# A 480-byte tile at the right edge of SBUF moves 14 expert weight buffers to multiples of 512 bytes

## The chip, the cores and the metric

One Trainium2 chip, one core of it. The metric is device time in microseconds (us) of one launch. TensorE, VectorE, ScalarE and GpSimd appear in profiles as PE (PEld for its weight loads), DVE, ACT and POOL; SP is SyncE, which here does nothing but issue DMA transfers and wait for what they need.

## The reference

One layer of a diffusion backbone in float32, with 512 latent tokens and 256 context tokens of width 1024. After a token mixer (Fourier branch, gated recurrent branch, merge, output projection) comes the sub-layer that matters here:

```
scores = softmax(h @ w_router)                      # 512 x 16
g, idx = top_k(scores^T, 64)                        # 64 tokens for each of 16 experts
hid = silu(xg @ w_gate[e]) * (xg @ w_up[e])         # 64 x 1536, w_gate and w_up: 1024 x 1536
out = (hid @ w_down[e]) * g                         # 64 x 1024, w_down: 1536 x 1024
x   = x + g2 * scatter_add(out);  return rmsnorm(x)
```

Each expert has three weight matrices of 6.29 MB, each used once. All 16 experts together read 302 MB.

## The kernel before

**The stages.** Up to 424 us of the profiled execution the kernel does the token mixer, then the output projection and the router (to 482 us), then the 16 experts one after the other (loop at L1160), and at the end the last sums, the norm and four stores (L1222 to L1301).

**The weights as units.** An expert's weights come in 24 units: 8 of `w_gate_e` (128 rows of 1536 floats), 8 of `w_up_e`, 8 of `w_down_e`. A unit is one DMA of 768 KB from HBM into a tile of 128 partitions by 1536 floats, so each partition receives one row of 6144 bytes. The list `units` (L826 to L830) holds 386 of them in the order of use. Only the last nine differ: unit 376 is the gain of the final norm, and 377 to 385 are the last expert's `w_down_e` in column blocks (rows of 2048 bytes in 377 to 380, of 1024 bytes in 381 to 385).

**The buffers.** `eload` (L835) issues the next unit and picks its buffer by the unit's number modulo 22. Buffers 0 to 13 belong to `rings[0]`, a pool opened at L825 on the right side of SBUF, where tiles are placed downward from the edge. Buffers 14 to 18 (`rings[1]`) and 19 (`rings[2]`) lie on the left side; 20 and 21 are two tiles held since before (`wd`, `we`):

```python
NR = (14, 5, 1)
m, i = n % (sum(NR) + 2), 0
while i < 3 and m >= NR[i]:
    m, i = m - NR[i], i + 1
t = rings[i].tile([P, DE], F32, tag="ew", bufs=NR[i], name=f"ew{n}") if i < 3 else held[m]
nc.sync.dma_start(t, src[P * q:P * q + P, :])
```

So in units, 14 transfers to the right ring are followed by 8 to the others, and so on: a turn of 22 units, while an expert takes 24.

**What orders the transfers.** All of them are issued by SP, in the order of `units`. A transfer waits until the unit that was in its buffer 22 units before has been used by TensorE. It also waits for one of eight semaphores in turn (named DMAHW0 to DMAHW7), that is, until the transfer eight before it has landed in all 128 partitions. So at most eight are under way.

**What uses them.** `up_gate` (L1108) multiplies each `w_gate_e` unit into the PSUM tile `G` and each `w_up_e` unit into `U` (L1116), and calls `eload` once per unit. Between units it runs hooks: the scatter of the expert before (L1132), the ranking of the expert two ahead. Odd experts also gather the tokens of the next two (L1088). ScalarE takes the silu of `G` at L1172, once per expert. `w_down_e` is multiplied at L1210, for the last expert at L1267.

**Two waits on ScalarE's queue.** In expert 2 (L1190) and in expert 14 (L1215) ScalarE issues a small DMA into `we` or `g2`. These use the same eight semaphores, so that SP stands until they have landed.

**Where the right ring lies.** Right of it is nothing before the change. The right side ends at byte 229,344 of a partition. The ring's lowest buffer starts at byte 143,328 = 279 x 512 + 480; buffers are 6144 = 12 x 512 bytes long, so all 14 start 480 bytes past a multiple of 512. The eight others start at multiples of 512, between bytes 70,144 and 133,632. The pool `rt` of the router (L865) lies left of the right ring. The four output tiles `os` (L1225) are cut from the right ring too.

Of the kernel before, what the change touches and what calls it, by code (L numbers as in the profile page):

```python
# [9 lines left out]
F32 = mybir.dt.float32  # L10
# [7 lines left out]
P = 128  # L18
# [58 lines left out]
def layer(ctx: ExitStack, tc: tile.TileContext, I, out):  # L77
# [4 lines left out]
    def open_pool(name, bufs=1, side="left", **kw):  # L82
        cm = tc.tile_pool(name=name, bufs=bufs, side=side, **kw)
        p = cm.__enter__()
        return p, lambda: cm.__exit__(None, None, None)

    def sb(name, side="left"):
        return open_pool(name, side=side, reuse_waits="tile")
# [733 lines left out]

    NR = (14, 5, 1)
    rings = [None] * 3
    rings[0], close_ra = sb("ra", "right")  # L825
    units = []  # L826
    for e in range(NE):
# [475 lines left out]
    close_rc()  # L1303
    close_rb()
    close_ra()
    close_stage()
    close_keep()

# [30 lines left out]
```

## Time and profile before

| | us |
|---|---|
| three runs, median | 1206.58 |
| lowest, highest | 1205.19, 1206.61 |
| the profiled execution, its own time | 1205.73 |
| the profiled execution, span from first to last instruction | 1203.9 |
| mean granted TensorE clock | 0.984 |

The span is the time of the profiled execution less 1.8 us that lie around it. All times below are counted from the span's start. The profile gives busy times by engine, the mean rate of the DMA engines by stretch, waits with what ended them, and instructions in order of time.

### The profile page before, as it was taken

The numbers are of one execution on the slowest core, as the hardware profiler recorded it, in microseconds if no ns is written. First come the engines' busy times: TensorE is split into PE (matmuls) and PEld (weight loads), VectorE is DVE, ScalarE is ACT, GpSimd is POOL, SyncE is SP. The second block draws the span as 40 slices with busy tenths as digits, with TensorE's granted clock in tenths as the row PEclk, the third lists the DMA queues.
The fourth block names the chain that finished last, engine by engine and source line by source line (L and its number), as shares of the span: only waits on it lengthen the run. The fifth ranks groups of instructions, "written<-read, shape, count | busy, mean of one in ns | idle before, by whom it ended". The sixth has DMA issues, their size and how long they took to land. (4 is left out here: it accounts for less than half of the span.)

```text
span 1203.9 us, 16716 instructions
## 1 busy us (share of the span) xinstructions
PE 1148.4 (95%) x6891; PEld 684.3 (57%) x6891; DVE 564.3 (47%) x1053; ACT 286.4 (24%) x448; POOL 112.9 (9%) x118
## 2 busy tenths in 40 slices
PE   8979988899999999999999999999999999999986
PEld 5768766588888897545445445445345345345333
DVE  5566899996776675233332332332232232232024
ACT  5443766644322223101001001001001001001004
POOL 5164443310000000000000000000000000000002
PEclk9989988999999999999999999999999999999998
DMA  8922011155555495899899999999999999999995
GB/s 308 300 89 88 18 53 53 35 173 177 188 180 191 149 390 206 313 379 418 356 422 419 418 420 421 418 419 421 420 417 421 421 418 418 422 421 418 419 400 211
DMA packets 115435, 368.01 MB, mean 306 GB/s; under 512 B 8912, under 2 KB 61656, under 8 KB 115232
## 3 DMA queue, kind: packets, MB, share of 16 engines
q1 hardware_dynamic: 112688, 363.52, 76.9%
q0 software_dynamic: 1088, 2.18, 0.6%
q10 hardware_dynamic: 1584, 1.25, 0.4%
q8 instruction: 54, 0.88, 0.3%
q14 instruction: 21, 0.17, 0.0%
HBM read 364.43 MB, written 2.10 MB: 304 GB/s over the span
## 5 line engine op out<-in xcount | busy, mean ns | idle before, releaser
L1116 PE MATMUL U<-ew,g 128*64 128x384 f32 x928 | 167.5, 494 | 8.7 <-DMA ew<-in_w_up_e 8.6
L1116 PE MATMUL G<-ew,g 128*64 128x384 f32 x960 | 171.7, 493 | 3.8 <-DMA ew<-in_w_gate_e 3.5
L1135 DVE TENSOR_TENSOR x<-x,sc 128x512 f32<-128x512 f32 x120 | 77.1, 684 | 104.2 <-PE sc L1132 104.2
L1116 PEld LDWEIGHTS G<-ew,g 128*64 128x64 f32 x960 | 62.8, 136 | 87.0 <-issue 62.6
L1116 PEld LDWEIGHTS U<-ew,g 128*64 128x64 f32 x928 | 60.0, 136 | 90.6 <-issue 56.9
L1247 POOL TENSOR_TENSOR o<-x,ew 128x512 f32<-128x512 f32 (+1 forms) x8 | 7.8, 1003 | 926.7 <-ACT o L1243 926.7
L1213 DVE SCALAR_TENSOR_TENSOR wc<-Y,gc,g 128x512 f32<-128x512 f32 x15 | 11.3, 751 | 148.6 <-PE Y L1210 148.6
L1210 PE MATMUL Y<-ew,wa 128*64 128x512 f32 x312 | 75.7, 598 | 2.2 <-ACT wa L1199 2.2
L1210 PE MATMUL Y<-ew,wd 128*64 128x512 f32 x324 | 77.5, 594 | 0.0
L1199 ACT COPY wa<-T 128x384 f32<-128x384 f32 x16 | 7.7, 479 | 254.2 <-PE T L1198 254.2
L230 DVE TENSOR_TENSOR wL<-raw,wH 128x1024 fp32r<-128x1024 f32 x48 | 62.9, 1341 | 2.0 <-ACT wH L229 1.6
L1172 ACT ACTIVATE wc<-G 128x768 f32<-128x768 f32 x16 | 13.0, 811 | 181.7 <-PE G L1116 181.7
L1210 PEld LDWEIGHTS Y<-ew,wd 128*64 128x64 f32 x324 | 24.2, 137 | 49.1 <-issue 41.7
L1088 PEld LDWEIGHTS xg<-wa,xn 128*128 128x128 f32 x448 | 51.1, 192 | 0.2
L1088 PE MATMUL xg<-wa,xn 128*128 128x128 f32 x448 | 51.2, 275 | 0.0
L1054 DVE TENSOR_SCALAR wc<-wa,score 128x128 bf16<-128x128 f32 (+3 forms) x63 | 24.0, 381 | 56.7 <-ACT wa L1047 56.7
L1210 PEld LDWEIGHTS Y<-ew,wa 128*64 128x64 f32 x312 | 21.8, 136 | 45.0 <-issue 34.6
L1216 ACT CAST wb<-wc 128x512 fp32r<-128x512 f32 x15 | 9.3, 619 | 156.1 <-DVE wc L1213 156.1
L674 PE MATMUL ga<-u,gw 128*128 128x512 f32 x64 | 36.0, 645 | 10.0 <-issue 9.9
L1132 PEld LDWEIGHTS sc<-wb 64*128 64x128 f32 x240 | 23.6, 184 | 35.9 <-issue 35.9
L229 ACT CAST wH<-raw 128x1024 fp32r<-128x1024 f32 x38 | 37.9, 1045 | 17.8 <-PE zO L426 9.9
L699 POOL TENSOR_TENSOR th<-tp,th 128x768 f32<-128x768 f32 x16 | 35.0, 2206 | 49.2 <-DVE tp L698 49.2
(360 smaller groups left out, 2183.9 us busy)
## 6 DMA issues: line engine op xcount, KB each, us to landing
ew<-in_w_gate_e SPq DMA_DIRECT2D x120, 768.0 KB, 14.9
ew<-in_w_up_e SPq DMA_DIRECT2D x116, 768.0 KB, 14.9
ew<-in_w_down_e SPq DMA_DIRECT2D x113, 768.0 KB, 14.9
raw<-in_w_ada SPq DMA_DIRECT2D x24, 1024.0 KB, 5.4
raw<-in_w_in SPq DMA_DIRECT2D x16, 1024.0 KB, 4.9
wd<-in_w_down_e SPq DMA_DIRECT2D x7, 768.0 KB, 12.3
we<-in_w_down_e SPq DMA_DIRECT2D x7, 768.0 KB, 12.9
wd<-in_w_up_e SPq DMA_DIRECT2D x6, 768.0 KB, 14.6
```

The costliest lines, as they stand in the source:

```text
L229: (copy or act.copy)(wH[:, a], raw[:, a])
L230: dve.tensor_sub(wL[:, a], raw[:, a], wH[:, a].bitcast(F32))
L674: pe.matmul(gf[:, 512:1024], gw[:, d, i, :], u[:, TC:TA], start=True, stop=True)
L699: pool.tensor_tensor(b, s, b, op=OP.mult)
L1054: dve.tensor_scalar(GT[c][:, 0:m], sB[:, 0:m], s, None, op0=OP.is_lt)
L1088: pe.matmul(a[k // 4][:, P * (k % 4) + q.start:P * (k % 4) + q.stop], XN[n // 2][:, n % 2, P * k:P * k + P], oh[:, n, q], start=n == 0, st ...
L1116: pe.matmul(t[64 * f:64 * f + 64, n, 0:384], xg[:, k, c:c + CAP], w[:, o:o + 384], start=k == 0, stop=k == KD - 1, tile_position=(0, 64 * f))
L1132: pe.matmul(a[dh][:, c], w, v, start=j == 0, stop=j == 1, tile_position=(64 * dh, 0))
L1135: dve.tensor_add(xs, xs, a[dh])
L1172: act.activation(v3(sl), G[:, :, 0:384], AF.Silu)
L1210: pe.matmul(yp[64 * dh:64 * dh + 64, :], hT[j // 3][:, j % 3, 64 * f:64 * f + 64], w[:, 512 * i:512 * i + 512], start=f == 0 and j == 0, s ...
L1213: dve.scalar_tensor_tensor(y, yp, gc[:, e % 3:e % 3 + 1], g2, op0=OP.mult, op1=OP.mult)
```

## The change

A pool of its own, opened on the right side just before the ring, with one tile of 120 floats (480 bytes) per partition. Nothing reads or writes it.

```diff
     NR = (14, 5, 1)
     rings = [None] * 3
+    edge, close_edge = open_pool("edge", side="right")
+    edge.tile([P, 120], F32, name="edge")
     rings[0], close_ra = sb("ra", "right")
...
     close_ra()
+    close_edge()
     close_stage()
```

The 14 buffers, the pool `rt` and the tiles `os` move 480 bytes down. The lowest buffer now starts at byte 142,848 = 279 x 512, and all 22 buffers start at multiples of 512. No instruction is added, removed or put elsewhere in its engine's order. What lay in that part of SBUF earlier (tiles of the mixer) now borders differently on the ring, and one wait moves. On SP, at the first loads of the right ring (`ew8` is unit 8; the names in brackets are semaphores: of the DMA queue, of TensorE, of GpSimd), before the change:

```order
L861 DMA ew6_3180<-in_w_gate_e 128x1536 [waits DMAHW7_49,PE_49]
L861 DMA ew7_3182<-in_w_gate_e 128x1536 [waits DMAHW0_49]
L861 DMA ew8_3184<-in_w_up_e 128x1536 [waits DMAHW1_49]
L861 DMA ew9_3186<-in_w_up_e 128x1536 [waits DMAHW2_49,PE_49,Pool_49]
L861 DMA ew10_3188<-in_w_up_e 128x1536 [waits DMASW5_49,DMASW4_49,DMASW6_49,DMASW3_49,DMASW7_49,DMASW2_49,DMAHW3_49,DMASW1_49,DMASW0_49]
```

The same place after it, two source lines further down:

```order
L863 DMA ew6_3184<-in_w_gate_e 128x1536 [waits DMAHW7_49,PE_49]
L863 DMA ew7_3186<-in_w_gate_e 128x1536 [waits DMAHW0_49]
L863 DMA ew8_3188<-in_w_up_e 128x1536 [waits DMAHW1_49,PE_49,Pool_49]
L863 DMA ew9_3190<-in_w_up_e 128x1536 [waits DMAHW2_49]
L863 DMA ew10_3192<-in_w_up_e 128x1536 [waits DMASW5_49,DMASW4_49,DMASW6_49,DMASW3_49,DMASW7_49,DMASW2_49,DMAHW3_49,DMASW1_49,DMASW0_49]
```

The wait for the earlier users of that memory on TensorE and GpSimd stands one transfer earlier, at unit 8 in place of unit 9.

## Rows read from the trace of the kernel before

**Rows 1.** The page, parts 1 and 2: busy times, DMA rate in 40 slices.

```profile
PE 1148.4 (95%) x6891; PEld 684.3 (57%) x6891; DVE 564.3 (47%) x1053; ACT 286.4 (24%) x448; POOL 112.9 (9%) x118
...
GB/s 308 300 89 88 18 53 53 35 173 177 188 180 191 149 390 206 313 379 418 356 422 419 418 420 421 418 419 421 420 417 421 421 418 418 422 421 418 419 400 211
```

**Rows 2.** Timeline of ACT, experts 2, 6, 10 and 14: start us, us, instruction.

```profile
589.18 0.81 ACT L1172 ACTIVATE wc<-G 128x768 f32<-128x768 f32 x1 [11.44 <-PE G L1116]
...
756.12 0.81 ACT L1172 ACTIVATE wc<-G 128x768 f32<-128x768 f32 x1 [11.44 <-PE G L1116]
...
932.13 0.81 ACT L1172 ACTIVATE wc<-G 128x768 f32<-128x768 f32 x1 [11.44 <-PE G L1116]
...
1113.11 0.81 ACT L1172 ACTIVATE wc<-G 128x768 f32<-128x768 f32 x1 [11.44 <-PE G L1116]
```

**Rows 3.** Waits of PEld, 602 to 780 us: us in total, times, longest.

```profile
PEld U L1116 <- DMA ew<-in_w_down_e: 0.7, 4, 0.2
```

**Rows 4.** Waits of PEld, 780 to 1172 us, same columns.

```profile
PEld U L1116 <- DMA ew<-in_w_up_e: 30.4, 37, 1.1
...
PEld G L1116 <- DMA ew<-in_w_gate_e: 17.3, 20, 1.5
```

**Rows 5.** Waits of SP's queue, 600 to 1140 us, same columns.

```profile
SPq L861 <- DMA ew<-in_w_gate_e: 128.6, 86, 2.9
```

**Rows 6.** Timeline of SP: start of a group, us to its end, transfers in it.

```profile
628.62 13.56 SPq L861 DMA_DIRECT2D ew<-in_w_gate_e  x8
...
843.40 9.79 SPq L859 DMA_DIRECT2D ew<-in_w_down_e  x6
...
862.25 5.82 SPq L861 DMA_DIRECT2D ew<-in_w_gate_e  x4
...
884.54 13.58 SPq L859 DMA_DIRECT2D ew<-in_w_down_e  x8
...
1126.96 15.47 SPq L861 DMA_DIRECT2D ew<-in_w_gate_e  x8
```

**Rows 7.** Windows of 4 us: busy times, then PEclk, DMA share, GB/s.

```profile
852.00:856.00 4.00, 4.00 (x43) 1.87 (x40) 1.54 (x3) 0.00 (x0) 0.00 (x0) 1.00 1.02 411
856.00:860.00 4.00, 3.83 (x20) 1.80 (x22) 1.45 (x3) 0.88 (x2) 0.00 (x0) 1.00 1.02 419
860.00:864.00 4.00, 4.00 (x18) 1.19 (x14) 0.00 (x0) 0.00 (x0) 0.00 (x0) 1.00 1.01 421
864.00:868.00 4.00, 4.00 (x15) 1.14 (x16) 0.00 (x0) 0.00 (x0) 0.00 (x0) 1.00 1.02 427
868.00:872.00 4.00, 3.69 (x18) 1.10 (x16) 1.51 (x3) 0.62 (x1) 0.00 (x0) 1.00 1.02 427
872.00:876.00 4.00, 3.90 (x28) 1.66 (x26) 1.29 (x2) 0.00 (x0) 0.00 (x0) 1.00 1.01 424
876.00:880.00 4.00, 3.90 (x28) 1.51 (x24) 1.29 (x2) 0.00 (x0) 0.00 (x0) 1.00 1.02 420
880.00:884.00 4.00, 3.85 (x28) 1.52 (x24) 1.28 (x2) 0.00 (x0) 0.00 (x0) 1.00 1.01 415
```

**Rows 8.** Windows of 17.5 us, same columns.

```profile
839.70:857.20 17.50, 17.34 (x128) 8.27 (x126) 8.13 (x20) 2.03 (x4) 0.00 (x0) 1.00 1.02 416
860.20:877.70 17.50, 17.09 (x88) 5.88 (x86) 3.17 (x6) 0.62 (x1) 0.00 (x0) 1.00 1.01 424
```

**Rows 9.** Waits of SP's queue, 540 to 600 us.

```profile
SPq L861 <- DMA we<-g: 13.4, 1, 13.4
```

**Rows 10.** Timeline of SP, 540 to 620 us.

```profile
593.33 3.97 SPq L861 DMA_DIRECT2D ew<-in_w_gate_e  x8
```

**Rows 11.** Timeline of PE, last expert: last unit of up, first of the 1024-byte rows.

```profile
1170.84 1.51 PE L1116 MATMUL U<-ew,g 128*64 128x384 f32 x8 [0.38 <-DMA ew<-in_w_up_e]
...
1182.65 0.83 PE L1267 MATMUL Y<-ew,wa 128*64 128x256 f32 x5 [0.36 <-DMA ew<-in_w_down_e]
```

**Rows 12.** Window between the first loads and the next ones.

```profile
455.00:468.00 13.00, 13.00 (x132) 12.30 (x131) 6.43 (x17) 3.49 (x10) 0.00 (x0) 1.00 0.02 6
```

## The prediction

> **What bounds the kernel now.** I read the page first, then the experts one by one on ScalarE's timeline, then the waits on both sides of the weight transfers, and last the DMA rate in short windows.
>
> The page shows TensorE busy for 95% of the span [rows 1], which looks like a TensorE kernel. The experts' times say otherwise. The silu of the gate comes once per expert, and since odd experts also gather, the experts are to be counted in pairs. From expert 2 to expert 6 it takes 756.12 - 589.18 = 166.94 us, 83.5 us per pair; from expert 10 to 14 it takes 180.98 us, 90.5 us per pair [rows 2]. The same instructions take 7 us more per pair late in the run. The waits say why: between 602 and 780 us the longest of TensorE's weight loads' waits for a DMA is 0.7 us in all, between 780 and 1172 us it is 30.4 us for up and 17.3 us for gate [rows 3, 4]. So TensorE sets the pace until about 780 us, living on what was loaded ahead, and the weight transfers set it from there to the last expert.
>
> The transfers themselves never rest in either stretch. From the 21st slice to the 38th the DMA rate stays at 417 to 422 GB/s [rows 1], and SP, which issues a transfer when the one eight before has landed, waits for landings and for nothing else that matters [rows 5]. So from about 600 us the end of the kernel is the end of the transfers plus a tail: a shorter transfer moves it, and TensorE's floor is 83.5 us per pair against 90.5.
>
> **What a transfer costs by its buffer.** In the steady stretch an issue on SP follows a landing, so the issues' spacing is the landings' spacing. Units 210 to 215 are issued at 843.40 to 853.19 us in a group of six; with 0.33 us for the issue itself that is (9.79 - 0.33) / 5 = 1.89 us apiece, and the landings that release them are of units 202 to 207, buffers 4 to 9 of the right ring. Units 220 to 223 come (5.82 - 0.33) / 3 = 1.83 us apart, released by units 212 to 215, buffers 14 to 17, which lie at multiples of 512 already [rows 6]. So the trace of before contains the experiment: 14 buffers off the multiple land at 1.89 us, 8 buffers on it at 1.83 us. The whole turn, unit 210 to unit 232, takes 884.54 - 843.40 = 41.14 us [rows 6].
>
> But the landing's gain is not the rate's gain. The windows count what the DMA engines take up, and there the fast stretch (421 to 427 GB/s) runs from about 858 to 878 us and the rest is near 415 [rows 7], in longer windows 424 against 416 [rows 8]. At 425 GB/s a unit of 786,432 bytes takes 1.850 us, and 20 us hold 11 units, though only 8 of the 22 buffers are on the multiple. I read this as two limits in a row with some slack between: taking up costs 1.85 us per unit whatever the buffer; landing costs 1.89 off the multiple, less than 1.85 on it. While the off ones land, the slack fills; while the 8 on it land at 1.83 they empty it, and the first three off ones go in at full rate again. Both add up: 11 x 1.85 + 11 x 1.89 = 41.1 and 8 x 1.83 + 14 x 1.89 = 41.1.
>
> **The change, part by part.** *The 14 buffers at the multiple:* all 22 units of a turn then go at 1.85 us, with nothing left to catch up: 22 x 1.850 = 40.70 us in place of 41.14, so 0.44 us per turn. Turns that count: the transfers have a fresh start at unit 72, when SP has stood 13.4 us for the small transfer that ScalarE issues in expert 2 and goes on at 593.33 us [rows 9, 10]. That time is set by TensorE, so nothing gained before it counts. From there to unit 375, the last whole unit, are 302 spacings after the first landing, 13.7 turns: 13.7 x 0.44 = **6.0 us**. What the turns lose beside this stays: from unit 96 at 628.62 to unit 360 at 1126.96 us twelve turns take 498.34 us, 41.53 each [rows 6], so 0.39 us per turn goes to single late landings that no buffer explains.
>
> *The last blocks.* Units 377 to 381 land in the right ring too, in rows of 2048 and 1024 bytes, between the last unit of up, used at 1170.84, and the first of the 1024-byte rows, used at 1182.65 us, both upon landing [rows 11]. No row of before shows such short rows on the multiple. Below: nothing. Above: the same 0.06 us per unit for 48 more rows, thus 0.06 / 8 = 0.008 us per row, as each of the 16 DMA engines has 8 of a unit's 128 rows; a unit in 2048-byte rows has 24 on it, one in 1024-byte rows 48, so 4 x 0.19 + 0.38 = 1.1 us. Taking up is a limit there as well, so I take the middle, **0.5 us**. After unit 381 the tail is arithmetic and stays.
>
> *The output tiles and `rt`:* stores of four tiles at the end, 0 to 0.2 us; I take **0.1**. *The moved wait:* unit 8 of the first loads now waits for old users of its memory. SP is not seen waiting there for them, and after the first 14 loads the DMA engines idle anyway at 6 GB/s from 455 to 468 us [rows 12]; cost 0, and at most nothing, since that idle stretch covers it. *TensorE:* its work stays, and nothing late takes the place of the landings, because 88.8 us per pair (48 units at 1.85) is still above 83.5.
>
> Sum: 6.0 + 0.5 + 0.1 = 6.6 us. Against the profiled execution's own 1205.73 us this gives 1199.1; that execution stands 0.85 us below the median of the three runs (1206.58), from which it would be 1200.0. I forecast **1199.6 us**, between the two, and 1197 to 1202 if the reading above is right.
>
> **A rule on the other side.** The rows above show 415 to 427 GB/s from HBM into SBUF. The Trainium skill, "DMA: Bandwidth & Descriptors", section "Where 436 GB/s comes from", says that for such transfers the HBM side binds at about 358 GB/s, so that nothing on the SBUF side would matter; by that the sum would be 0. The trace does not agree: the rate is higher and follows the buffer.
>
> **The rivals.**
>
> *The landing's gain in full.* If taking up is not a limit of its own, all 22 units go at 1.83: 22 x 1.83 = 40.26, 0.88 us per turn, 12.1 us, with 0.5 to 1.1 for the blocks 12.6 to 13.3 us: about 1193. For it: 1.83 is what is seen at landing. Against: 425 GB/s holds for 20 us and is not exceeded while the eight on the multiple are under way. Chance 0.14. The Trainium skill, same page, section "How a descriptor splits into AXI transactions", bears on it: a run that starts off a 256-byte boundary pays for the unused bytes before it. For 6144 bytes starting 224 past a boundary that is, by estimate, 199 beats in place of 192, 3.6%; 1.89 / 1.83 is 3.3%, so the landings agree, and by the rule alone the time would be this rival's.
>
> *It is the place, not the multiple.* The 14 buffers that land at 1.89 all lie above byte 143,000, the eight that land at 1.83 all below 140,000. If the upper part of SBUF is slower for another reason, 480 bytes change nothing: 1205.7 to 1206.6. Nothing in the trace excludes it, as it has no saturated transfer to an upper tile on the multiple; it has no mechanism in the rows either. Chance 0.10. A smaller part of the gain, 2.4 to 4 us, for instance because late landings grow: 0.08.
>
> *Slower: all on the multiple collide.* Today at most 8 transfers on the multiple follow each other. If 22 that start alike met in the same places of SBUF, a unit could cost as much as an off one throughout: 22 x 1.89 = 41.58, 0.44 us more per turn, 6.0 us: 1212. It decides from a mean above 41.14 / 22 = 1.870 us per unit. Against: eight such transfers are already under way together at 872 us, and that is within the fast stretch at 424 GB/s [rows 7]. Chance 0.04.
>
> **How the numbers follow.** Main case 0.64. About 0.2% (2.4 us) is what a measurement of this kernel can tell from no change. Faster by more: 0.64 + 0.14 + 0.08 = 0.86; within it 0.10; slower 0.04. The range has to hold 8 in 10: from 1193.0, which takes in the landing's gain, to 1203.0, which takes in most of the smaller gain and leaves out the place and the collision.
>
> **What would show it.** Windows of 17.5 us anywhere from 640 to 1120 us at 422 to 426 GB/s, without the turn's rise and fall; SP's issues 1.85 us apart for all buffers; the first waits of TensorE for a DMA some 30 us later than 780 (the transfers then fall behind by 7 - 48 x 0.02 = 6 us per pair); experts 10 to 14 at about 89.5 us per pair. Wrong would be: issues at 1.83 throughout (first rival), the rise and fall unchanged (the place), or a rate below 417 (collision).

## The result, and the profile after

| | before | after |
|---|---|---|
| median of six runs each, us | 1206.59 | 1199.97 |
| lowest, highest | 1204.87, 1209.7 | 1197.88, 1203.5 |
| the profiled execution, own time | 1205.73 | 1197.88 |
| its span | 1203.9 | 1196.1 |
| mean granted TensorE clock | 0.984 | 0.986 |

After to before is 0.9946, with a 95% interval of 0.9926 to 0.9967: faster by 6.6 us. The forecast was 1199.6 us, in a range of 1193 to 1203.

The page after, the rows that answer to [rows 1]:

```profile
PE 1142.9 (96%) x6873; PEld 683.5 (57%) x6891; DVE 564.5 (47%) x1053; ACT 286.3 (24%) x448; POOL 112.9 (9%) x118
...
GB/s 312 298 92 88 18 53 53 35 161 192 172 180 210 141 374 201 311 377 424 351 423 424 423 424 424 423 424 424 424 424 423 425 423 424 424 424 423 424 416 219
```

The busy times say nothing of the change. The rate says all of it: the slices that stood at 417 to 422 GB/s now stand at 423 to 425. The windows show what that is made of (the two of [rows 8]; then the 528 us from 602 us on):

```profile
839.70:857.20 17.50, 17.28 (x123) 7.94 (x122) 7.38 (x19) 1.79 (x4) 0.00 (x0) 1.00 1.02 425
860.20:877.70 17.50, 17.05 (x96) 6.21 (x95) 4.26 (x8) 0.62 (x1) 0.00 (x0) 1.00 1.01 422
...
602.00:1130.00 528.00, 517.05 (x3333) 242.50 (x3344) 158.64 (x348) 44.82 (x85) 0.00 (x0) 1.00 1.02 424
```

The turn's rise and fall (416, then 424) is gone. SP's timeline after shows the same in the issues:

```profile
592.70 3.97 SPq L863 DMA_DIRECT2D ew<-in_w_gate_e  x8
...
627.70 13.16 SPq L863 DMA_DIRECT2D ew<-in_w_gate_e  x8
...
836.58 13.22 SPq L861 DMA_DIRECT2D ew<-in_w_down_e  x8
...
858.71 5.89 SPq L863 DMA_DIRECT2D ew<-in_w_gate_e  x4
...
880.91 13.30 SPq L861 DMA_DIRECT2D ew<-in_w_down_e  x8
...
1120.38 15.13 SPq L863 DMA_DIRECT2D ew<-in_w_gate_e  x8
```

The group at 880.91 us begins with unit 232, as does that at 884.54 us in [rows 6]: released by landings in the right ring, its issues stood (13.58 - 0.33) / 7 = 1.89 us apart before and stand (13.30 - 0.33) / 7 = 1.85 us apart now. The four at 858.71 us, released by the other buffers, went from 1.83 to (5.89 - 0.33) / 3 = 1.85 us. So the transfers that were off the multiple became faster and the others a little slower, as two limits in a row would have it. Over the twelve turns from unit 96 to 360, spacings of 1.7 to 2.0 us alone, the mean behind a landing in the right ring went from 1.889 to 1.846 us, behind one in the other buffers from 1.835 to 1.846.

TensorE's waits after, from 780 to 1166 us (compare [rows 4]), and the silu on ScalarE in experts 6 to 10 and 14:

```profile
PEld U L1118 <- DMA ew<-in_w_up_e: 22.7, 28, 1.3
...
PEld G L1118 <- DMA ew<-in_w_gate_e: 16.0, 19, 1.4
```

```profile
755.48 0.81 ACT L1174 ACTIVATE wc<-G 128x768 f32<-128x768 f32 x1 [11.45 <-PE G L1118]
793.72 0.81 ACT L1174 ACTIVATE wc<-G 128x768 f32<-128x768 f32 x1 [11.44 <-PE G L1118]
839.22 0.81 ACT L1174 ACTIVATE wc<-G 128x768 f32<-128x768 f32 x1 [11.44 <-PE G L1118]
880.67 0.81 ACT L1174 ACTIVATE wc<-G 128x768 f32<-128x768 f32 x1 [13.04 <-PE G L1118]
928.22 0.81 ACT L1174 ACTIVATE wc<-G 128x768 f32<-128x768 f32 x1 [11.44 <-PE G L1118]
...
1107.32 0.81 ACT L1174 ACTIVATE wc<-G 128x768 f32<-128x768 f32 x1 [11.45 <-PE G L1118]
```

TensorE waits less and later. An undisturbed pair still takes 83.5 us, as from 755.48 to 839.22 (83.74); the loss begins in the next pair. From expert 10 to 14 it takes (1107.32 - 928.22) / 2 = 89.55 us per pair, where it took 90.5 [rows 2].

The ends of the two traces show where the 7.8 us of span went:

```profile
1163.61 1.51 PE L1118 MATMUL U<-ew,g 128*64 128x384 f32 x8 [0.34 <-DMA ew<-in_w_up_e]
...
1174.72 0.83 PE L1269 MATMUL Y<-ew,wa 128*64 128x256 f32 x5 [0.19 <-DMA ew<-in_w_down_e]
```

| stretch, us | before | after | difference |
|---|---|---|---|
| start to the issue of unit 72 | 593.33 | 592.70 | -0.63 |
| unit 72 to unit 96 | 35.29 | 35.00 | -0.29 |
| unit 96 to unit 360, 12 turns | 498.34 | 492.68 | -5.66 |
| unit 360 to TensorE's last unit of up | 43.88 | 43.23 | -0.65 |
| to the first 1024-byte rows | 11.81 | 11.11 | -0.70 |
| to the end of the span | 21.25 | 21.38 | +0.13 |

The first row is not the change's: unit 72 goes out when the small transfer of expert 2 has landed, which comes behind the compute of that expert, and from 480 to 593 us of the trace of before TensorE's weight loads wait less than 1 us in all for a DMA. The row differs from execution to execution. From unit 72 on, 610.57 us became 603.40.

### The profile page after: what moved, and what is told of

It is laid out like the page before. It is cut to its first block, busy times and chain, and to the rows that moved or that the text cites. A ratio compares the mean times of both kernels' runs of the same rounds, so it can differ in the third digit from the quotient of the medians.

```text
span 1196.1 us, 16698 instructions
## 1 busy us (share of the span) xinstructions
PE 1142.9 (96%) x6873; PEld 683.5 (57%) x6891; DVE 564.5 (47%) x1053; ACT 286.3 (24%) x448; POOL 112.9 (9%) x118
```

## The experiments

**Theory:** a transfer into SBUF costs more at landing where its rows start off a boundary; all 22 buffers on it run at the limit of taking up. **Rivals:** the gain depends on the bytes before the start that are paid for, not on being off; it is the place in SBUF; there is no second limit, each transfer simply has its price. Below, a buffer is called off where its rows start off a multiple of 256 bytes, and on where they start at one.

All ratios below are to runs of the kernel before on the same chip (medians 1206.98 us beside e1 to e4, 1205.95 beside e5 to e8, one run of 1206.48 beside e9 and e10). Two numbers of the profile are steadier than the total, since they leave out the first 590 us: the twelve turns from unit 96 to 360, and the time from unit 72 to the end of the span. Both are of one execution each. In the four kernels with all 22 buffers on (the change, e1, e7, e8) the twelve turns take 492.68 to 492.77 us, which shows how steady they are.

| right ring starts (bytes past a multiple of 256) | 12 turns | from unit 72 | median us; ratio [95%] |
|---|---|---|---|
| 224 (before) | 498.34 | 610.57 | |
| 0 (the change) | 492.68 | 603.40 | 1199.97; 0.9946 [0.9926, 0.9967] |
| 0, odd multiple of 256 (e1) | 492.69 | 603.64 | 1199.85; 0.9945 [0.9932, 0.9958] |
| 32 (e2) | 498.44 | 610.76 | 1206.85; 0.9994 [0.9974, 1.0014] |
| 64 (e9) | 496.96 | 609.10 | one run, 1205.89 |
| 128 (e3) | 496.01 | 608.68 | 1204.52; 0.9986 [0.9976, 0.9996] |
| 192 (e10) | 497.45 | 609.46 | one run, 1196.70 |
| 20 of 22 buffers at 224 (e4) | 502.99 | 615.86 | 1211.25; 1.0041 [1.0027, 1.0054] |
| first 7 of a turn at 224 (e5) | 494.59 | 606.08 | 1202.4; 0.9963 [0.9949, 0.9977] |
| every second of 14 at 224 (e6) | 493.36 | 604.70 | 1200.26; 0.9946 [0.9932, 0.9960] |

### Which boundary, and what is paid: e1, e2, e3, e9, e10

Each changes only the size of the edge tile, and with it where the 14 buffers start:

```diff
-    edge.tile([P, 120], F32, name="edge")
+    edge.tile([P, 56], F32, name="edge")   # e1: 512 k + 256
+    edge.tile([P, 112], F32, name="edge")  # e2: 512 k + 32
+    edge.tile([P, 88], F32, name="edge")   # e3: 512 k + 128
+    edge.tile([P, 104], F32, name="edge")  # e9: 512 k + 64
+    edge.tile([P, 72], F32, name="edge")   # e10: 512 k + 192
```

> The extra tile has 224 bytes, so the 14 right buffers start 256 bytes past a multiple of 512. Theory 'boundaries of 256 bytes': nothing differs from the change, the rate stays level at 422 to 426 GB/s in every window of 17.5 us, about 6.6 us under the kernel before (1200 beside 1206.6). Rival 'only 512 will do': windows rise and fall between 415 and 425 GB/s as before, and the time is that of before within 1 us.

> The extra tile has 448 bytes, so the 14 right buffers start 32 bytes past a multiple of 512, also past one of 256. Theory 'the bytes between the boundary below and the start are paid for': 32 bytes in 6144 are 0.5%, against 224 bytes and 3.3% in the kernel before; landing would cost 1.83 x 1.005 = 1.84 us per unit, under the 1.85 of taking up, so the rate stays level at 422 to 426 GB/s and the time is that of the change, about 6.6 us under before. Rival 'every start off the boundary costs one more piece, whatever the distance': 1.89 us per unit landed, 415 to 425 GB/s by turns, the time of before within 1 us.

> The extra tile has 352 bytes, so the 14 right buffers start 128 bytes past a multiple of 512. Theory of the bytes paid for: 128 in 6144 are 2.1%, landing 1.83 x 1.021 = 1.868 us, just over taking up: a turn of 22 units takes 14 x 1.868 + 8 x 1.83 = 40.8 us, where 22 x 1.85 is 40.7, so at most 0.1 us per turn over the change, 0 to 1.4 us in all; windows between 421 and 425 GB/s. Rival 'one more piece whatever the distance': the time of before within 1 us, windows 415 to 425.

At 256 (e1) the time is that of the change, so a multiple of 256 bytes is enough here. At 32 (e2) it is that of before. SP's timelines of e1 and e2, at units 96, 232 and 360:

```profile
629.97 13.19 SPq L863 DMA_DIRECT2D ew<-in_w_gate_e  x8
...
882.95 13.28 SPq L861 DMA_DIRECT2D ew<-in_w_down_e  x8
...
1122.66 15.13 SPq L863 DMA_DIRECT2D ew<-in_w_gate_e  x8
```

```profile
628.81 13.56 SPq L863 DMA_DIRECT2D ew<-in_w_gate_e  x8
...
884.88 13.57 SPq L861 DMA_DIRECT2D ew<-in_w_down_e  x8
...
1127.25 15.48 SPq L863 DMA_DIRECT2D ew<-in_w_gate_e  x8
```

(13.57 - 0.33) / 7 = 1.89 us for a unit at 32, the same as at 224. The windows of e2 have the old rise and fall:

```profile
839.70:857.20 17.50, 17.50 (x128) 8.32 (x126) 8.08 (x20) 1.75 (x3) 0.00 (x0) 1.00 1.02 416
860.20:877.70 17.50, 17.08 (x86) 5.73 (x84) 2.82 (x6) 0.62 (x1) 0.00 (x0) 1.00 1.02 425
```

So the price is not the bytes between the boundary and the start: at 32 it would have been a seventh of that at 224. What costs is that the row starts off the boundary at all. At 128 (e3) it costs somewhat less: 496.01 us, (13.50 - 0.33) / 7 = 1.88 us per unit:

```profile
884.46 13.50 SPq L861 DMA_DIRECT2D ew<-in_w_down_e  x8
```

Neither theory had that (the median, 1204.52 us, is 2.5 below before, where the one expected at most 1.4 over the change and the other the time of before within 1), so two kernels followed between these starts, each run once:

> The edge tile is 416 bytes, so the 14 buffers start 64 past a multiple of 256 (a row of 6144 bytes then begins with a piece of 192 bytes and ends with one of 64). The runs before gave twelve turns of 492.7 us at 0 past, 498.4 at 32 and at 224, 496.0 at 128. Theory A (only a piece of 32 bytes costs the last tenth, every other split costs the same): like 128, twelve turns about 496.0 us, landings of the 14 at 1.881 us. Theory B (the cost falls smoothly from 32 towards 128): between, about 497.5 us, landings 1.887. Theory C (128 is the exception, all other splits cost the same): 498.4 us, landings 1.89.

> The edge tile is 288 bytes, so the 14 buffers start 192 past a multiple of 256 (first piece 64 bytes, last 192). All three theories of the run at 64 past expect the same here as there: A 496.0 us for twelve turns, B about 497.5, C 498.4. If the first piece decided rather than the split, 192 would lie away from 64, towards 224 (498.4), while 64 would lie towards 0.

```profile
630.21 13.50 SPq L863 DMA_DIRECT2D ew<-in_w_gate_e  x8
...
885.49 13.53 SPq L861 DMA_DIRECT2D ew<-in_w_down_e  x8
...
1127.17 15.39 SPq L863 DMA_DIRECT2D ew<-in_w_gate_e  x8
```

```profile
620.48 13.51 SPq L863 DMA_DIRECT2D ew<-in_w_gate_e  x8
...
876.07 13.56 SPq L861 DMA_DIRECT2D ew<-in_w_down_e  x8
...
1117.93 15.39 SPq L863 DMA_DIRECT2D ew<-in_w_gate_e  x8
```

497.0 us at 64 (e9, the first fence) and 497.5 at 192 (e10): between 32 and 128, as theory B had it at 192 and between A and B at 64. A row that starts off the boundary has two ends shorter than 256 bytes, one ahead of its first boundary and one behind its last, together 256. Ordered by the shorter of the two, twelve turns cost 5.7 us above the change at 32 bytes (both sides), 4.3 and 4.8 at 64, 3.3 at 128, nothing at 0. More than half is there at every start tried off the boundary; the rest grows as the shorter end shrinks. That the first end alone decides is ruled out by 32 and 224, which cost the same. Each of these is one execution, and the 0.5 us between 64 and 192 is not to be read.

The whole time of e10's one run was 1196.7 us, 9.8 under the run of before beside it. That is not its start in SBUF: its turns are slow, and from unit 72 on it takes 609.46 us. It gained ahead of the experts. The window of 60 to 90 us, before and in e10 (after the busy times: granted clock, DMA share, GB/s):

```profile
60.00:90.00 30.00, 23.74 (x118) 18.42 (x119) 18.24 (x27) 13.89 (x30) 18.82 (x35) 0.83 0.28 92
```

```profile
60.00:90.00 30.00, 28.54 (x177) 23.07 (x177) 19.09 (x32) 19.63 (x43) 25.91 (x40) 1.00 0.26 84
```

Before, the granted clock was 0.83 on the mean there, so it lay at the lower of its levels (1.2 GHz) for part of the window, while TensorE was busy 23.74 of 30 us; in e10 it stayed at 2.4 GHz. Why this one execution kept it was not tried, and that the clock is the whole of the gain is not shown. It does show why a difference of 5 us is better read from the stretch that it concerns.

### The place or the start: e4

The kernel before, with the 480-byte tile ahead of the left rings instead, so that `rings[0]` stays off and `rings[1]` and `rings[2]` go off too: 20 of 22 buffers.

```diff
+    low, close_low = open_pool("low")
+    low.tile([P, 120], F32, name="low")
     rings[1], close_rb = sb("rb")
...
     close_rb()
+    close_low()
```

> The kernel before, with an unused tile of 480 bytes ahead of the left ring: 20 of the 22 buffers start 480 bytes past a multiple of 512, two at one. Theory 'the start decides': a turn takes about 20 x 1.89 + 2 x 1.83 = 41.46 us in place of 41.14, 13.7 turns, 4.4 us more than before: about 1211; windows level at 415 to 417 GB/s. Rival 'the place decides' (buffers high in SBUF are slow, low ones are not): the time of before within 1 us, windows still up to 424.

```profile
631.49 13.57 SPq L861 DMA_DIRECT2D ew<-in_w_gate_e  x8
...
1134.48 15.46 SPq L861 DMA_DIRECT2D ew<-in_w_gate_e  x8
```

1211.25 us, slower than before by 0.41% (4.3 us, where 4.4 were expected); twelve turns 502.99 us. The windows of e4 no longer rise:

```profile
839.70:857.20 17.50, 17.50 (x118) 7.91 (x116) 6.97 (x17) 1.40 (x2) 0.00 (x0) 1.00 1.02 415
860.20:877.70 17.50, 16.96 (x74) 5.87 (x72) 3.16 (x7) 1.50 (x3) 0.00 (x0) 1.00 1.02 417
```

The left buffers, moved off, become as slow as the right ones were (1.89 to 1.90 us, the medians by buffer of the issues that their landings release); the right ones, moved on by the change, as fast as the left ones. The start decides, not the place.

### One price per transfer, or two limits: e5, e6

The change, with the right ring split into two pools of seven on either side of the edge tile: `ringo` stays off, `rings[0]` is on. e5 uses the off ones as the first seven of a turn, e6 every second one:

```diff
+    ringo, close_ro = sb("ro", "right")
     edge, close_edge = open_pool("edge", side="right")
...
+        if i == 0:
+            t = (ringo if m < 7 else rings[0]).tile([P, DE], F32, tag="ew", bufs=7, name=f"ew{n}")
```

(In e6, `m % 2` in place of `m < 7`; the tiles `os` are cut from `rings[0]` with its seven buffers.) Both have seven off buffers, so by a price per transfer both would give the same time.

> The right ring in two pools of seven, the first seven units of a turn start 480 bytes past a multiple of 512, the other 15 at one. Theory 'taking up at 1.85 us, landing at 1.89 or 1.83, with slack for three or four units between': of 7 x 0.04 = 0.28 us that the seven lose, about 0.13 goes into the slack, so a turn takes 40.7 + 0.15 = 40.85 us and the time lies 2 us over the change, about 1202. Rival 'each unit off the boundary costs its share of the 0.43 us that fourteen cost': 0.21 us per turn, 2.9 us over the change, about 1203. The two lie close; the next run parts them.

> The same two pools of seven, but units go to them in turn, so that one off the boundary is followed by one on it through the right ring. Theory of the two limits with slack: a pair lands in 1.89 + 1.83 = 3.72 us, about what two units take to be taken up (3.70), so the slack swallows it: a turn of 40.7 to 40.8 us, the time of the change within 1 us (1200 to 1201), rates level at 422 to 426 GB/s. Rival 'each unit off the boundary costs its share': as in the run before, 2.9 us over the change, about 1203.

e5: 1202.4 us, twelve turns 494.59, so 0.16 us per turn over the change (0.15 by the two limits, 0.21 by a price per transfer). e6: 1200.26 us, twelve turns 493.36, so 0.06 us per turn over it (0 to 0.1, or again 0.21). The windows of e5 (first fence) and e6:

```profile
839.70:857.20 17.50, 17.28 (x127) 8.33 (x126) 8.13 (x20) 2.09 (x4) 0.00 (x0) 1.00 1.02 422
```

```profile
839.70:857.20 17.50, 17.28 (x125) 8.16 (x124) 7.55 (x20) 2.27 (x4) 0.00 (x0) 1.00 1.02 424
```

In e6 the landings alternate between 1.88 to 1.89 and 1.84 us (medians by buffer of the issues that they release), yet the DMA engines take up 424 GB/s: an off one followed by an on one costs next to nothing, as their mean, 1.86 us, is all but the 1.85 of taking up. In a row of seven (e5) the slack runs out: the seven land 1.89 us apart, the five behind them 1.83 while they catch up, the rest 1.83 to 1.86. A plain price per transfer is ruled out, since the same seven buffers off cost less than half as much in e6. Two limits in a row fit all three kernels; what the two limits are made of is not shown.

### The two stands on ScalarE's queue: e7, e8

Not part of the change. [rows 9] had put 13.4 us of SP's wait to the small transfer of expert 2, and after the change it is still there (SP's waits from 540 to 600 us, then the window in which the transfers run dry):

```profile
SPq L863 <- DMA we<-g: 12.9, 1, 12.9
```

```profile
588.00:592.00 4.00, 4.00 (x28) 1.74 (x26) 0.88 (x3) 1.40 (x2) 0.00 (x0) 1.00 0.28 92
```

e7 is the change with that transfer issued by GpSimd, whose semaphores SP does not share; e8 also moves the one of expert 14:

```diff
-                nc.scalar.dma_start(g20[64 * q:64 * q + 64, :], g2[0:64, :])
+                pool.dma_start(g20[64 * q:64 * q + 64, :], g2[0:64, :])   # e7, e8
...
-            nc.scalar.dma_start(g2[0:64, :], g2[64:128, :])
+            pool.dma_start(g2[0:64, :], g2[64:128, :])                    # e8
```

> The change, with the small transfer of expert 2 (L1190 of the kernel before) issued by GpSimd, whose transfers use other semaphores, so that SP no longer stands 12.9 us at unit 72. Theory 'from unit 72 the transfers set the end, and start anew at a time that TensorE sets': the rate hole of 588 to 596 us (92 and 231 GB/s in two windows of 4 us, 4.9 us of transfer time) closes and the end comes 4 to 5 us earlier than with the change: about 1195. Rival 'the buffers would have kept SP waiting there anyway': the time of the change within 1 us.

> As the run before, and the small transfer of expert 14 (L1215 of the kernel before) on GpSimd too, so that SP does not stand 4.7 us at unit 369 either. Theory: at unit 369 eight transfers are still under way, no landing comes late for it, so 0 to 1 us less than the run before, about 1194.5. Rival 'that stand costs its 4.7 us': about 1190.

e7: 1194.21 us, ratio 0.9900 [0.9883, 0.9917]. The window of e7 and its issue of unit 72:

```profile
588.00:592.00 4.00, 4.00 (x28) 1.72 (x24) 0.77 (x2) 0.81 (x1) 0.00 (x0) 1.00 1.02 427
```

```profile
582.12 11.74 SPq L863 DMA_DIRECT2D ew<-in_w_gate_e  x8
```

Unit 72 goes 10.6 us sooner and the transfers no longer run dry. From the first expert's silu table load to the end of the span it takes 1191.5 - 500.60 = 690.9 us; without e7's edit, 1196.1 - 498.85 = 697.25. So this stand had cost 6.35 us by these two executions, nearly as much as the whole change gives; the medians lie 5.8 us apart, in sets of runs at different times. The hole in the rate, from which 4 to 5 us were expected, does not account for all of it, and the rest has no cause shown.

e8: 1192.22 us, ratio 0.9877 [0.9858, 0.9895], the best of all kernels here. Its second move cannot be told from e7: the intervals overlap, the median of e8 is of four runs only, and in the profile the same stretch takes 1195.2 - 504.27 = 690.9 us. SP's wait that it takes away, from the waits of e7 from 1110 to 1190 us:

```profile
SPq L863 <- DMA g<-g: 4.6, 1, 4.6
```

That wait is gone in e8, and from unit 360 to the last unit of up the trace becomes no shorter (43.23 us in e7, 43.36 in e8). Eight transfers under way last 8 x 1.85 = 14.8 us; a stand of 4.6 us does not empty them.

## Why the prediction was right

- *The bound.* Right. The end followed the transfers: what the transfers gained from unit 72 on, 7.3 us with the last blocks, arrived at the end of the span (7.2), though TensorE shows 96% busy. TensorE's floor of 83.5 us per pair did not bind; late pairs take 89.55 us (predicted 89.5).
- *The main term, 6.0 us from unit 72 to the end of the 768 KB units.* Measured 0.29 + 5.66 + 0.65 = 6.60. Per turn it was 5.66 / 12 = 0.47 us for 0.44: the turn takes 41.06 us where 40.70 + 0.39 = 41.09 was expected. Late single landings did not grow; they come to 41.06 - 40.70 = 0.36 us per turn. Most of that is three gaps: units 166, 250 and 339 go out 3.1 us after the unit ahead (units 165, 249 and 339 before, 3.4 to 3.5 us). Neither the prediction nor a run says what makes them. Of the 0.6 us that the term is short, about 0.35 arise after unit 360 and have no cause shown.
- *The two limits.* Right, and this chose between 1199 and 1193. No window of 17.5 us read in the trace after or in an experiment is above 426 GB/s, and e6 shows the slack by itself. (That 425 GB/s "is not exceeded" holds of such windows; two of 4 us in [rows 7] have 427.) The rival that gave the landing's gain in full would have had issues 1.83 us apart throughout and, with the same late landings, turns of 40.26 + 0.39 = 40.65 us; the mean spacing is 1.846 us and a turn takes 41.06. Single groups come close to the rival's figure, as that at 627.70 us with (13.16 - 0.33) / 7 = 1.83, so the turns decide and not a group.
- *The last blocks, 0.5 us between 0 and 1.1.* Measured 11.81 - 11.11 = 0.70. It is no chance of one execution: the four kernels with all buffers on take 11.03 to 11.11 us here, the six with the whole right ring off 11.63 to 11.92.
- *Output tiles and `rt`, 0.1 us.* Measured nothing (+0.13 us to the end).
- *The moved wait, 0.* Right: unit 8 goes out 1.89 us after unit 7 (1.85 before), and unit 13, the last of the first 14, at 440.19 us (441.16 before), ahead of the idle stretch. SP now waits 1.5 us for TensorE at the first loads, where it waited for a landing.
- *First waits of TensorE some 30 us later than 780.* Right in direction, and a little more: before, the loss begins ahead of expert 8's silu, now between those of expert 8 and 9 (41.45 us for 38.24). From 780 to 820 us the waits for up fell from 5.0 us to 0.9 (before, then after), and 840 us was reached with no more:

```profile
PEld U L1116 <- DMA ew<-in_w_up_e: 5.0, 6, 1.1
...
PEld U L1118 <- DMA ew<-in_w_up_e: 0.9, 2, 0.7
```

- *The rivals.* The place (0.10) fell with the result, which moved the buffers by 480 bytes and gained all the same, and with e4. The smaller gain (0.08) fell too: 6.6 us, and late landings did not grow. The collision (0.04): 22 transfers that start alike run at 424 GB/s. The rule that HBM binds at about 358 GB/s, which the prediction cited from the Trainium skill, "DMA: Bandwidth & Descriptors", "Where 436 GB/s comes from", does not hold here: one core kept 424 GB/s for 528 us. The section has the figure from a stack's rate divided between two cores, and this program uses one.
- *The rule behind the first rival.* By the same page's section "How a descriptor splits into AXI transactions" the unused bytes before an unaligned start cost beats. That agreed with the landing times at 224 past a boundary, but e2 pays in full at 32 past, where those bytes are a seventh. The section is written of reads; here the unaligned side is the one written to.

That the total came out 0.4 us from the forecast is in part luck. The interval of the ratio leaves the gain anywhere from 4.0 to 8.9 us, and in the profiled executions it is 7.2 us from unit 72 on: the main term was 0.6 and the last blocks 0.2 us too small, the output tiles 0.2 too large. What the runs bear out is the mechanism and the gain per turn, 0.47 us for 0.44.

## What to carry to other kernels

Look at where the rows of a DMA start in SBUF: an edge or a pool that ends off a multiple of 256 bytes shifts every buffer placed against it (here the right edge, at byte 229,344), and 14 of 22 buffers off it cost 1.1% of the twelve turns and 0.55% of the time. Such a price shows in a trace that has both kinds of buffer: compare the landings by buffer, then ask in long windows what the engines take up, since here the slower of the two set the time. And where one queue issues all the transfers, look for a small transfer elsewhere that shares its semaphores: moving one off (e7) gave nearly as much again.

## What the hardware showed that was not expected

- A row of 6144 bytes cost more at every start tried off a multiple of 256 bytes in SBUF (32, 64, 128, 192 and 224 past), and most where one end is 32 bytes: 1.89 us per 768 KB unit at 32 and 224 past, 1.88 at 128, against 1.83 at which the on ones among them land.
- 256 is enough; 512 k + 256 is as good as 512 k (492.69 and 492.68 us for twelve turns).
- Off and on transfers in alternation run at all but the full rate (e6): half of the right ring could have stayed off for 0.06 us per turn.
- The mean granted clock of the window from 60 to 90 us, in the mixer, was 0.66 in the profiled execution of e8, 0.77 to 0.83 in those of ten others, before and after among them, and 1.00 in e10. The first unit of expert 0 was multiplied at 487.09 us in e8, 482.32 before, 474.43 in e10. So up to 13 us of a single time are decided before any weight of an expert is used.
